# A two-layer diffusion trunk: other products for the first 256 feed-forward columns, two thirds of the second layer's modulation on TensorE, other buffers for the last down weights

## The chip, the core and the metric

One NeuronCore of one Trainium2 chip runs the whole program, in one launch, on fp32 inputs. The metric is the device time of the core in microseconds (us). One execution was also profiled; its rows stand below.

## What is computed

Two trunk layers run over 640 tokens (512 sample tokens in tiles 0 to 3, 128 prompt tokens in tile 4). What matters here of the reference, for each layer:

```python
mod = silu(cond) @ w_mod + b_mod                     # six vectors of 1024, per condition
sh1, sc1, ga1, sh2, sc2, ga2 = split(mod, 6)
h = rmsnorm(x, g_pre1) * (1 + sc1) + sh1
proj = h @ w_in                                      # inputs of four mixers, and the gates
mix = sum_m(sigmoid(gate_m) * (branch_m @ w_br_m)) @ w_o
x = x + ga1 * rmsnorm(mix, g_post1)
h2 = rmsnorm(x, g_pre2) * (1 + sc2) + sh2
gt, up = split(h2 @ w_up, 2)                         # 2 x 2816 columns
x = x + ga2 * rmsnorm((silu(gt) * up) @ w_down, g_post2)
```

## The kernel before, in words

**Products.** Every fp32 operand is split into a high and a low part (ScalarE copies the high part, VectorE subtracts), and a product is the sum of three matmuls: high by high, high by low, low by high (`mm`, L135; transposes are L140). `wchunk` (L143 to 152) loads weights into a `raw` buffer (three of them) and splits them into `whi` and `wlo`.

**Feed-forward.** The 22 blocks of 128 columns are taken in `FGROUPS`: a group of two blocks, then five groups of four. For each pair of blocks `up_pair` (L1321) is called for the gate half and for the up half of `w_up`. It computes 256 columns by 640 tokens with Strassen's seven products instead of eight: each is a sum of weight blocks (made on VectorE, L1333, and split, L1352) by a sum of activation blocks. The tokens are cut into halves of 320 (`TH`), the depth of 1024 into two halves, so a product has 12 matmuls of 320 columns and a pair 84. The activation blocks lie in `hb`: `hb[1]` and `hb[2]` hold the first token half, `hb[3]` the second half's lower depth, and 5, 6, 7, 4 are sums that `combine` (L1294) makes tile by tile once the tiles 2, 3 and 4 of the second half are normed. After a group's pairs comes its down projection (10 outputs of 512 columns for five token tiles and two column halves).

**The head.** `ffn_head` (L1400) runs behind the output projection of the mixers and fills the time in which `post` (L1230) and `prenorm` (L361; its Square is L369) of the last tiles finish. It starts three pairs, (0,0), (0,1) and (1,0), as generators with products 1 and 2 of each, which need `hb[1]` and `hb[2]` alone; between them it pops from `self.late` the norms of tiles 3 and 4, and then the three `combine`s. The other products follow in `ffn`.

**Modulation.** A layer's six vectors come in three groups of 2048 columns. `mod_group` (L281) does a group on TensorE: 16 loads of 512 KB into `V` (two buffers), each followed by four matmuls of 32 rows by 256 columns, in four column strips of the array (`keep`, L218). `mod_group_v` (L305) does a group on VectorE: 64 operations of 128 by 512 (L319, L321), and a few closing matmuls. Layer 0's groups 1 and 2 go by `mod_group` during `gates(2)`. Layer 1's three groups go by `mod_group_v` as a filler in layer 0's feed-forward: one step for each `up_pair`, three for each weight chunk of a down projection (`step`, L1418).

**The last group.** For the last group of a layer all of the down weights are held, so that tile by tile (L1472 ff.) both column halves are finished, added up (L1481) and passed to `post`: the residual, the next layer's first norm, and the store of the output. The weights are two chunks in `whi`/`wlo` for the first column half, one more for the second, and two single blocks that `wchunk1` (L154) puts into `tg` and `cv`. `tg` has two buffers, and `post` also needs one: L1238 writes `tg<-acc,oh`.

A tile framework places the instructions: it orders each engine by data and buffer dependences, so a buffer that comes free later delays all that is to write it. All loads are issued by SyncE, in order.

Of the kernel before, what the change touches and what calls it, by code (L numbers as in the profile page):

```python
# [10 lines left out]
F32R = mybir.dt.float32r  # L11
# [7 lines left out]
KT = 8  # L19
# [10 lines left out]
HEAD = 1, 2, 5, 6, 3, 7, 4  # L30
# [9 lines left out]
TG = 648  # L40
# [67 lines left out]
class Step:  # L108
# [44 lines left out]

    def wchunk1(self, src, tags):  # L154

        nc = self.nc
        raw = self.t("raw", [128, 1024])[:, :512]
        self.dma.dma_start(raw, src.rearrange("p k c -> p (k c)"))
        hi, lo = (self.t(t, [128, TG], F32R)[:, :512] for t in tags)
        nc.scalar.activation(hi, raw, AF.Copy)  # L160
        nc.vector.tensor_tensor(lo, raw, hi, op=ALU.subtract)
        return hi.unsqueeze(1), lo.unsqueeze(1)
# [1067 lines left out]
    def post(self, i, t0, t1, s, G, xsrc, xdst, M, which, hh2):  # L1230
# [15 lines left out]
        if hh2 is not None:  # L1246
# [18 lines left out]
    def new_hb(self):  # L1265

        t = [self.t(n, [128, KT, NTOK], F32R).rearrange("p a t -> p (a t)") for n in ("hhi", "hlo")]
        blk = lambda x, j: x[:, j * SLOT:j * SLOT + SLOT].rearrange("p (k t) -> p k t", k=4)
        return {p: (blk(t[0], j), blk(t[1], j)) for j, p in enumerate((1, 2, 3, 5))}
# [51 lines left out]
    def up_pair(self, l, c0, hb, silu, E, order, tag="raw"):  # L1321
# [5 lines left out]
        for q in range(2):  # L1327
            r = self.t(tag, [128, 1024 if tag == "raw" else SLOT])[:, :1024].rearrange("p (k c) -> p k c", k=4)
# [3 lines left out]
        s1 = None  # L1332
        tt = lambda o, x, y, op: nc.vector.tensor_tensor(o, x, y, op=op)  # L1333
        done = set()

        def operand(p):
            nonlocal s1
            if p == 5 or p in (6, 7, 3) and 5 not in done:
                s1 = self.t("dt", [128, 512]).rearrange("p (k c) -> p k c", k=4)
                tt(s1, A21, A22, ALU.add)  # L1340
                done.add(5)
            if p in (6, 7, 3) and 6 not in done:
                tt(A21, A11, A21, ALU.subtract)
                tt(A11, s1, A11, ALU.subtract)
                done.add(6)
            if p == 3:
# [12 lines left out]
        for p in order:  # L1359
# [25 lines left out]
            if p in (3, 4) and {3, 4} <= set(order[:order.index(p) + 1]):  # L1385
# [6 lines left out]
            yield  # L1392
# [6 lines left out]

    def ffn_head(self, l, hb):  # L1400

        head = {}
        late = self.late
        self.late = []
# [202 lines left out]
```

## Time and profile before

| | us |
|---|---|
| three runs | 2465.18, 2472.25, 2473.31 (median 2472.25) |
| the profiled execution | 2471.39 |
| its span, first to last instruction | 2469.6 |
| TensorE busy | 2305.1 |
| VectorE busy | 1670.7 |
| ScalarE busy | 998.5 |
| GpSimd busy | 259.4 |

The mean granted clock of TensorE is 0.970 of full speed. TensorE is the busiest engine, but busy time is an average over stages: a stage's own limit is read from windows of it. A row of a window gives, after its stretch, each engine's busy time with its instructions in brackets, then the granted clock, the DMA engines' share and the rate. PEld is TensorE's weight load.

### The profile page before, as it was taken

How to read it: one execution, taken by the hardware profiler on the slowest of the kernel's cores; microseconds unless marked ns; L12 is line 12 of the kernel's file. 1: busy time of each engine (PE TensorE's matmuls, PEld its weight loads, DVE VectorE, ACT ScalarE, POOL GpSimd, SP SyncE). 2: the span in 40 equal slices, each digit the busy share in tenths (PEclk: the TensorE clock that was granted, in tenths of full speed). 3: DMA queues.
4: the chain of work that ended last, by engine and by line, in shares of the span. 5: the costliest groups of instructions: out<-in, count | busy, mean ns of one | idle time of the engine just before them, and what ended most of it. 6: DMA issues, size and time to landing. Idle time of an engine off the chain costs nothing. (4 is left out here: it accounts for less than half of the span.)

```text
span 2469.6 us, 38694 instructions
## 1 busy us (share of the span) xinstructions
PE 2305.1 (93%) x14822; PEld 2027.0 (82%) x14822; DVE 1670.7 (68%) x3546; ACT 998.5 (40%) x2076; POOL 259.4 (11%) x320
## 2 busy tenths in 40 slices
PE   7999999999996898889989999999999969999996
PEld 6877688979875877779978887889799759999995
DVE  4653788476458899997666646884764587666765
ACT  4442553232236524234344544532322356334442
POOL 0000203131030000000011011031310300000001
PEclk9999999999998999999989999999999979999998
DMA  9647033325342354553344121234253422222222
GB/s 264 162 126 226 29 91 87 98 58 129 123 146 91 111 167 137 168 158 97 94 122 112 37 57 51 86 88 101 58 145 110 148 86 77 86 83 89 86 85 94
DMA packets 316585, 269.45 MB, mean 109 GB/s; under 512 B 72096, under 2 KB 267296, under 8 KB 316400
## 3 DMA queue, kind: packets, MB, share of 16 engines
q1 hardware_dynamic: 316400, 266.98, 36.3%
q8 instruction: 117, 1.92, 0.3%
q14 instruction: 68, 0.56, 0.1%
HBM read 234.73 MB, written 32.20 MB: 108 GB/s over the span
## 5 line engine op out<-in xcount | busy, mean ns | idle before, releaser
L135 PE MATMUL psg<-hhi,wlo 128*128 128x384 f32 (+2 forms) x1632 | 509.8, 321 | 9.4 <-ACT wlo L1352 4.4
L135 PE MATMUL psg<-hhi,whi 128*128 128x384 f32 (+2 forms) x1600 | 502.3, 321 | 7.1 <-DVE tg L1186 5.6
L135 PE MATMUL psg<-hlo,whi 128*128 128x384 f32 (+2 forms) x1520 | 486.9, 320 | 0.0
L151 DVE TENSOR_TENSOR wlo<-raw,whi 128x1024 fp32r<-128x1024 f32 (+1 forms) x170 | 212.7, 1252 | 177.7 <-ACT whi L150 175.0
L135 PEld LDWEIGHTS psg<-hhi,wlo 128*128 128x128 f32 x1632 | 308.3, 191 | 23.0 <-issue 6.9
L135 PEld LDWEIGHTS psg<-hhi,whi 128*128 128x128 f32 x1600 | 300.9, 190 | 20.6 <-issue 8.1
L135 PEld LDWEIGHTS psg<-hlo,whi 128*128 128x128 f32 x1520 | 288.5, 190 | 16.2 <-issue 14.3
L150 ACT ACTIVATE whi<-raw 128x1024 fp32r<-128x1024 f32 (+1 forms) x170 | 179.6, 1058 | 212.5 <-PE psg L135 161.6
L135 PE MATMUL pss<-hhi,whi 128*128 128x320 f32 x512 | 133.9, 330 | 29.0 <-ACT whi L1352 13.4
L135 PE MATMUL pss<-hhi,wlo 128*128 128x320 f32 x544 | 134.1, 314 | 7.6 <-ACT hhi L1307 4.9
L1155 ACT ACTIVATE tg<-psg 128x384 f32<-128x384 f32 (+1 forms) x128 | 55.0, 431 | 196.1 <-PE psg L135 177.5
L321 DVE SCALAR_TENSOR_TENSOR P<-V,cs,P 128x512 f32<-128x512 f32 x168 | 119.2, 749 | 16.8 <-DMA V<-in_w_mod 16.3
L1352 ACT ACTIVATE wlo<-raw 128x512 fp32r<-128x512 f32 x118 | 73.1, 630 | 131.1 <-PE psc L135 63.7
L135 PE MATMUL psg<-oh,whi 128*128 128x384 f32 (+1 forms) x512 | 119.8, 318 | 4.3 <-DVE tg L1186 4.0
L135 PEld LDWEIGHTS pss<-hhi,whi 128*128 128x128 f32 x512 | 94.6, 202 | 34.1 <-DVE whi L1333 15.1
L135 PE MATMUL psg<-whi,U 128*128 128x512 f32 x356 | 117.2, 392 | 0.0
L1333 DVE TENSOR_TENSOR wlo<-raw,wlo 128x512 fp32r<-128x512 f32 x118 | 81.2, 689 | 47.7 <-ACT wlo L1352 47.1
L1188 POOL TENSOR_TENSOR acc<-acc,tg 128x640 f32<-128x640 f32 x48 | 85.2, 1779 | 248.7 <-DVE tg L1186 248.7
L135 PEld LDWEIGHTS pss<-hhi,wlo 128*128 128x128 f32 x544 | 95.5, 192 | 9.9 <-ACT hhi L1307 5.7
L1333 DVE TENSOR_TENSOR whi<-raw,whi 128x512 fp32r<-128x512 f32 x122 | 83.6, 689 | 29.3 <-ACT whi L1352 29.3
L135 PE MATMUL pss<-whi,U 128*128 128x512 f32 x304 | 101.8, 391 | 1.0 <-ACT U L167 1.0
L135 PEld LDWEIGHTS psg<-oh,whi 128*128 128x128 f32 x512 | 86.1, 190 | 12.9 <-DVE tg L1186 7.8
(578 smaller groups left out, 5114.1 us busy)
## 6 DMA issues: line engine op xcount, KB each, us to landing
raw<-in_w_in SPq DMA_DIRECT2D x86, 512.0 KB
raw<-in_w_up SPq DMA_DIRECT2D x80, 512.0 KB
V<-in_w_mod SPq DMA_DIRECT2D x96, 256.0 KB
raw<-in_w_down SPq DMA_DIRECT2D x42, 512.0 KB
V<-in_w_mod SPq DMA_DIRECT2D x32, 512.0 KB
raw<-in_w_o SPq DMA_DIRECT2D x16, 512.0 KB
xs<-V SPq DMA_DIRECT2D x15, 512.0 KB
V<-xs SPq DMA_DIRECT2D x15, 512.0 KB
```

Source lines behind the costliest of these rows:

```text
L135: return self.nc.tensor.matmul(out, lhsT, rhs, start=start, stop=stop, skip_group_check=True)
L150: nc.scalar.activation(hi, raw[:, :a * b], AF.Copy)
L151: nc.vector.tensor_tensor(lo, raw[:, :a * b], hi, op=ALU.subtract)
L321: nc.vector.scalar_tensor_tensor(acc[:, s, :], raw, self.cs[:, k, s:s + 1], acc[:, s, :], op0=ALU.mult, op1=ALU.add)
L1155: self.nc.scalar.activation(tg[:, o:o + sz], p, AF.Tanh, scale=0.5)
L1188: nc.gpsimd.tensor_tensor(a, a, tg, op=ALU.add)
L1333: tt = lambda o, x, y, op: nc.vector.tensor_tensor(o, x, y, op=op)
L1352: nc.scalar.activation(hi, src, AF.Copy)
```

## The change

1. **The first 256 columns.** `ffn_head` no longer starts three pairs. It loads four chunks of 128 columns (blocks 0 and 1, gate and up) with `wchunk`, and multiplies each with the first token half (`fm_half`, 24 matmuls of 320 columns); norms of tiles 3 and 4 are popped after the first and the second. The new `ffn_first` then multiplies the same chunks with the second token half, from `hb[0]` (new, in two `U` buffers) and `hb[3]`, and pops a `combine` after each of the first three. Block products are eight here rather than seven, and pair (1,0) no longer begins in the head.
2. **Modulation.** In layer 0's feed-forward the filler is group 0 alone, one step for each `up_pair`. Groups 1 and 2 of layer 1 are done by `mod_group` in layer 1's `gates(2)`, as layer 0's are.
3. **The last weights.** The last group's fourth chunk goes whole into the two `T` buffers; `wchunk1` is gone, and with it the weights in `tg` and `cv`.
4. `norm_blocks` fills `hb[0]` too, and `more_hb` moves to the end of the head.

```diff
@@ post @@
-                self.late.append(lambda: (self.more_hb(hh2), self.combine(i, h32, hh2)))
+                self.late.append(lambda: self.combine(i, h32, hh2))
...
-                self.late.insert(2 * i - 6, lambda: self.h32.__setitem__(i, norm()))
+                self.late.insert(i - 3, lambda: self.h32.__setitem__(i, norm()))
@@ new_hb @@
+        hb[0] = tuple(self.t("U", [128, SLOT], F32R).rearrange("p (k t) -> p k t", k=4) for _ in range(2))
@@ norm_blocks @@
-                if second and q == 0:
-                    continue
-                hi, lo = hb[3 if second else 1 + q]
+                hi, lo = hb[3 * q if second else 1 + q]
@@ the head @@
+    def fm_half(self, out, w, b0, b1):
+        for k in range(KT):
+            for y, (a, b) in enumerate(((0, 0), (0, 1), (1, 0))):
+                self.mm(out, w[a][:, k, :], (b1 if k >= 4 else b0)[b][:, k % 4, :], k == 0 and y == 0, k == KT - 1 and y == 2)
...
     def ffn_head(self, l, hb):
-        for j, (n, up) in enumerate(((0, 0), (0, 1), (1, 0))):
-            E = self.pair_tiles(n, up)
-            g = self.up_pair(l, up * D_FF + n * 256, hb, not up, E, HEAD, ("raw", "U", "V")[j])
-            head[n, up] = g, E
-            next(g)
-            next(g)
-            if late:
-                late.pop(0)()
-        while late:
-            late.pop(0)()
+        for j, (n, up) in enumerate(((0, 0), (0, 1), (1, 0), (1, 1))):
+            ch = self.up_chunk(l, up * D_FF + n * 128, ("whi", "wlo") if j < 3 else ("oh", "oh"))
+            p = self.ps("s" if up else "g")[:, :TH]
+            self.fm_half(p, ch, hb[1], hb[2])
+            head[n, up] = ch, p
+            if j in (0, 1):
+                self.late.pop(0)()
+        self.more_hb(hb)
         return head
+    def ffn_first(self, head, hb):
...
+        for n in range(2):
+            out = {}
+            for up in range(2):
+                ch, p = head[n, up]
+                q = self.ps("s" if up else "g")[:, :TH]
+                self.fm_half(q, ch, hb[0], hb[3])
+                out[up] = (t1, p), (t2, q)
+                if self.late:
+                    self.late.pop(0)()
...
+            self.split(hi[:, n, :], lo[:, n, :], s)
@@ ffn @@
-            parts = {"hi": [], "lo": []}
+            parts = {"hi": [], "lo": []} if gi else self.ffn_first(head, hb)
...
                         ch = mk(k, co)
-                        step(3)
...
-            chs.append([(mk(0, 512), (0, 1), (0, 1))])
-            chs[1] += [(self.wchunk1(wd[:, f0 + k:f0 + k + 1, 512:1024], ("tg", "cv")), (0,), (k,)) for k in range(2, nf)]
+            chs = [[(mk(k, co, ("T", "T") if k and co else ("whi", "wlo")), (0, 1), (k, k + 1)) for k in range(0, nf, 2)]
+                   for co in (0, 512)]
@@ run @@
-            if l == 0:
-                self.bg = chain(*(self.mod_group(M, g, "c", "c") for g in (1, 2)))
+            self.bg = chain(*(self.mod_group(M, g, "c", "c") for g in (1, 2)))
...
-                filler = chain(*(self.mod_group_v(Mn, g, "o", "t") for g in range(3)))
+                filler = self.mod_group_v(Mn, 0, "o", "t")
```

How the change moves instructions shows at three places. In the rows below a name before the arrow is written, names behind it are read, and numbers tell buffers apart.

TensorE in the head of layer 0, before: the last of 48 matmuls on `hb[1]` and `hb[2]` (`hhi`, `hlo`), for two pairs, then the transposes of tile 3's norm (written to `pst` and `psc`), twelve more matmuls, the transposes of tile 4, and twelve more.

```order
L135 MATMUL pss_7750<-hhi_7103,whi_7747 128x320
L140 MATMUL pst_7704<-cst_63,P_7690 128x128 x4
L140 MATMUL psc_7705<-cst_63,P_7690 128x128 x4
L135 MATMUL psg_7791<-hhi_7103,wlo_7788 128x320
...
L135 MATMUL psg_7791<-hhi_7103,wlo_7788 128x320
L140 MATMUL pst_7836<-cst_63,P_7822 128x128 x4
L140 MATMUL psc_7837<-cst_63,P_7822 128x128 x4
L135 MATMUL pss_7808<-hhi_7103,whi_7805 128x320
```

TensorE at the same place now:

```order
L134 MATMUL psg_7794<-hhi_7103,wlo_7791 128x320
L139 MATMUL pst_7699<-cst_63,P_7685 128x128 x4
L139 MATMUL psc_7700<-cst_63,P_7685 128x128 x4
L134 MATMUL pss_7825<-hhi_7103,oh_7821 128x320
...
L134 MATMUL pss_7825<-hhi_7103,oh_7822 128x320
L139 MATMUL pst_7766<-cst_63,P_7752 128x128 x4
L139 MATMUL psc_7767<-cst_63,P_7752 128x128 x4
L134 MATMUL pss_7825<-hhi_7103,oh_7821 128x320
...
L134 MATMUL pss_7825<-hhi_7103,oh_7822 128x320
L134 MATMUL psg_7864<-U_7105,whi_7656 128x320
```

Of the first token half's 96 matmuls 72 now stand ahead of tile 3's transposes (48 before), and 18 more ahead of tile 4's (twelve before); from the row with `U` on come the products with the second token half.

VectorE in layer 0's feed-forward, with the filler (`P<-V,cs,P`) between operands of `up_pair`, before:

```order
L1333 TENSOR_TENSOR raw_8486<-raw_8486,raw_8484 128x4x128
L1333 TENSOR_TENSOR wlo_8593<-raw_8486,wlo_8593 128x512
L321 SCALAR_TENSOR_TENSOR P_8331<-V_8611,cs_218,P_8331 128x512
L1333 TENSOR_TENSOR whi_8577<-raw_8486,whi_8577 128x512
L1333 TENSOR_TENSOR tg_8483<-tg_8483 128x320
L321 SCALAR_TENSOR_TENSOR P_8331<-V_8611,cs_218,P_8331 128x512
L321 SCALAR_TENSOR_TENSOR P_8331<-V_8615,cs_218,P_8331 128x512
L1333 TENSOR_TENSOR tg_8482<-tg_8482,pss_8510 128x320
L321 SCALAR_TENSOR_TENSOR P_8331<-V_8615,cs_218,P_8331 128x512
```

and now:

```order
L310 SCALAR_TENSOR_TENSOR P_8249<-V_8387,cs_218,P_8249 128x512 x2
L310 SCALAR_TENSOR_TENSOR P_8249<-V_8529,cs_218,P_8249 128x512 x2
L1323 TENSOR_TENSOR wlo_8196<-raw_8121,wlo_8196 128x512
L310 SCALAR_TENSOR_TENSOR P_8249<-V_8533,cs_218,P_8249 128x512
L1323 TENSOR_TENSOR whi_8214<-raw_8123,whi_8214 128x512
L310 SCALAR_TENSOR_TENSOR P_8249<-V_8533,cs_218,P_8249 128x512
L1323 TENSOR_TENSOR wlo_8230<-raw_8123,wlo_8230 128x512
L310 SCALAR_TENSOR_TENSOR P_8249<-V_8663,cs_218,P_8249 128x512 x2
L1323 TENSOR_TENSOR whi_8264<-raw_8259,whi_8264 128x512
L1323 TENSOR_TENSOR dt_8263<-raw_8259,raw_8261 128x512
```

Line 310 is L321 in the numbering of before, L1323 is L1333. The filler's rows stand as close together as before, but there are 64 operations rather than 192: they reach from row 1180 to row 1350 of VectorE's order, those of before from row 1213 to row 1555. Between these ends now lie the first down projection, the whole of the next group (four `up_pair`s and its down projection) and three `up_pair`s more.

VectorE at the end of layer 1, before: the addition of the last tile's first half (`oh<-oh,psg`), and only then the L1238 of tiles 0 to 3, two at a time.

```order
L1481 TENSOR_TENSOR oh_19726<-oh_19726,psg_23313 128x512
L245 SCALAR_TENSOR_TENSOR rr_23297<-rs_u_23301,rr_23297 128x1
L1238 TENSOR_TENSOR tg_23135<-acc_19722,oh_23066 128x512
L1238 TENSOR_TENSOR tg_23188<-acc_19723,oh_23066 128x512
L1244 SCALAR_TENSOR_TENSOR V_23132<-tg_23135,rr_23138,V_23132 128x512
L1244 SCALAR_TENSOR_TENSOR V_23185<-tg_23188,rr_23191,V_23185 128x512
L1238 TENSOR_TENSOR tg_23241<-acc_19724,oh_23066 128x512
L1238 TENSOR_TENSOR tg_23294<-acc_19725,oh_23066 128x512
L1481 TENSOR_TENSOR oh_19726<-oh_19726,psg_23330 128x512
```

VectorE at the end of layer 1 now, tile 0 (L1484 is L1481, L1227 is L1238, L1232 and L1233 are L1243 and L1244):

```order
L1484 TENSOR_TENSOR acc_19557<-acc_19557,psg_22969 128x512
L1484 TENSOR_TENSOR acc_19557<-acc_19557,psg_22986 128x512
L1227 TENSOR_TENSOR tg_23003<-acc_19557,oh_22940 128x512
L1230 TENSOR_TENSOR ss_23007<-o_s_3487_22968 128x1
...
L1232 SCALAR_TENSOR_TENSOR V_23000<-acc_19557,rr_23006,V_23000 128x512
L1233 SCALAR_TENSOR_TENSOR V_23000<-tg_23003,rr_23006,V_23000 128x512
L1484 TENSOR_TENSOR acc_19558<-acc_19558,psg_23039 128x512
L1227 TENSOR_TENSOR tg_23056<-acc_19558,oh_22940 128x512
```

Tile 0's `tg` is now written, and its output finished, before tile 1's second half is added; in layer 0's last group it is the same.

## Rows read from the trace of the kernel before

**Rows 1.** The page, part 1: busy us, share of the span, instructions.
```profile
PE 2305.1 (93%) x14822; PEld 2027.0 (82%) x14822; DVE 1670.7 (68%) x3546; ACT 998.5 (40%) x2076; POOL 259.4 (11%) x320
```

**Rows 2.** Windows, layer 1, one group of four column blocks: engines' busy us, clock, DMA.
```profile
2112.90:2189.40 76.50, 76.50 (x458) 71.80 (x457) 51.59 (x81) 32.57 (x58) 0.00 (x0) 1.00 0.26 83
```

**Rows 3.** Windows, same columns: first down's end to last matmul, layers 0 and 1.
```profile
831.70:1277.70 446.00, 406.38 (x2316) 364.59 (x2315) 371.79 (x601) 167.36 (x304) 5.79 (x12) 0.97 0.42 132
2066.80:2447.00 380.20, 379.69 (x2256) 354.99 (x2255) 257.23 (x422) 165.73 (x303) 5.64 (x5) 1.00 0.26 81
```

**Rows 4.** The page, part 5: line, engine, tiles, count, busy, mean ns, idle before.
```profile
L321 DVE SCALAR_TENSOR_TENSOR P<-V,cs,P 128x512 f32<-128x512 f32 x168 | 119.2, 749 | 16.8 <-DMA V<-in_w_mod 16.3
```

**Rows 5.** Windows, same columns, layer 0's feed-forward with and without the filler.
```profile
1000.00:1100.00 100.00, 86.04 (x480) 74.77 (x481) 93.28 (x152) 32.75 (x59) 0.00 (x0) 0.98 0.49 154
1180.00:1260.00 80.00, 80.00 (x471) 74.06 (x470) 55.05 (x90) 35.15 (x65) 1.90 (x9) 1.00 0.32 98
```

**Rows 6.** Timeline, TensorE, head of layer 0: start, us, instruction, idle before and releaser.
```profile
763.31 0.57 PE L135 MATMUL psg<-hhi,wlo 128*128 128x320 f32 x2 [1.40 <-ACT hhi L1290]
...
770.71 0.31 PE L135 MATMUL pss<-hhi,whi 128*128 128x320 f32 x1
776.88 1.12 PE L140 MATMUL pst<-cst,P 128*128 128x128 f32 x4 [5.86 <-ACT P L369]
...
786.76 0.66 PE L140 MATMUL pst<-cst,P 128*128 128x128 f32 x4 [2.08 <-ACT P L369]
...
798.24 0.64 PE L135 MATMUL pss<-hlo,wlo 128*128 128x320 f32 x1 [0.58 <-DVE hlo L1303]
...
818.39 0.62 PE L135 MATMUL pss<-whi,U 128*128 128x512 f32 x2
...
831.68 0.31 PE L135 MATMUL pss<-hhi,wlo 128*128 128x320 f32 x1
```

**Rows 7.** Windows, heads of layers 0 and 1.
```profile
762.00:800.00 38.00, 20.42 (x96) 17.84 (x97) 35.16 (x92) 21.58 (x45) 0.76 (x1) 0.75 0.17 56
1996.00:2033.00 37.00, 19.99 (x90) 17.00 (x90) 33.31 (x89) 21.50 (x45) 0.76 (x1) 0.69 0.16 58
```

**Rows 8.** Chain of waits, layer 1: start, us, engine, tile, line, instructions.
```profile
2010.81 3.50 DMA V<-in_w_up
...
2150.72 3.51 PE psg L135 x24
```

**Rows 9.** Windows of line 218 alone, layer 0's gates.
```profile
130.00:245.00 115.00, 22.04 (x256) 6.61 (x256) 0.99 0.62 187
```

**Rows 10.** Line 218 there: what its engine waited for (us, times).
```profile
  DMA V<-in_w_mod: 7.4, 13
```

**Rows 11.** Timeline, TensorE, from layer 0's last matmul into layer 1.
```profile
1277.73 0.40 PE L135 MATMUL psg<-tg,U 128*128 128x512 f32 x1
1286.23 1.11 PE L140 MATMUL pst<-cst,P 128*128 128x128 f32 x4 [8.10 <-ACT P L369]
...
1290.37 0.78 PE L135 MATMUL psg<-whi,hhi 128*128 128x496 f32 x1 [2.17 <-ACT hhi L386]
```

**Rows 12.** Windows: start of layer 1's projection; after the last matmul.
```profile
1290.00:1318.00 28.00, 24.12 (x102) 17.97 (x102) 21.68 (x70) 20.00 (x37) 6.36 (x5) 0.88 0.37 126
2447.00:2469.60 22.60, 0.42 (x2) 0.00 (x0) 11.43 (x22) 0.72 (x2) 0.81 (x1) 0.57 0.53 186
```

**Rows 13.** Timeline, all engines, after layer 1's last matmul.
```profile
2446.77 2.19 DVE L1238 TENSOR_TENSOR tg<-acc,oh 128x512 f32<-128x512 f32 x2 [1.06 <-PE psg L135]
...
2451.41 0.68 DVE L1481 TENSOR_TENSOR oh<-oh,psg 128x512 f32<-128x512 f32 x1
...
2454.52 0.16 DVE L245 SCALAR_TENSOR_TENSOR rr<-rs_u,rr 128x1 f32<-128x1 f32 x1
...
2464.50 0.75 DVE L1243 SCALAR_TENSOR_TENSOR V<-oh,rr,V 128x512 f32<-128x512 f32 x1 [4.77 <-DMA V<-xs]
2465.95 0.33 SPq L1245 DMA_DIRECT2D out_y_prompt<-V  x1
```

More of the change, by code (lines that the diff above doesn't have):

```diff
@@ L1268, in new_hb @@
         blk = lambda x, j: x[:, j * SLOT:j * SLOT + SLOT].rearrange("p (k t) -> p k t", k=4)
-        return {p: (blk(t[0], j), blk(t[1], j)) for j, p in enumerate((1, 2, 3, 5))}
+        hb = {p: (blk(t[0], j), blk(t[1], j)) for j, p in enumerate((1, 2, 3, 5))}
+        hb[0] = tuple(self.t("U", [128, SLOT], F32R).rearrange("p (k t) -> p k t", k=4) for _ in range(2))
+        return hb
     def more_hb(self, hb):
@@ L1319, in combine, with up_pair @@
         parts(4, t6)
-    def up_pair(self, l, c0, hb, silu, E, order, tag="raw"):
+    def up_pair(self, l, c0, hb, silu, E):
         nc = self.nc
@@ L1331, in up_pair @@
         (A11, A21), (A12, A22) = ((r[:, :, 0:128], r[:, :, 128:256]) for r in raw)
-        s1 = None
+        s1 = self.t("dt", [128, 512]).rearrange("p (k c) -> p k c", k=4)
         tt = lambda o, x, y, op: nc.vector.tensor_tensor(o, x, y, op=op)
-        done = set()
         def operand(p):
-            nonlocal s1
-            if p == 5 or p in (6, 7, 3) and 5 not in done:
-                s1 = self.t("dt", [128, 512]).rearrange("p (k c) -> p k c", k=4)
+            if p == 5:
                 tt(s1, A21, A22, ALU.add)
-                done.add(5)
-            if p in (6, 7, 3) and 6 not in done:
+            elif p == 6:
                 tt(A21, A11, A21, ALU.subtract)
                 tt(A11, s1, A11, ALU.subtract)
-                done.add(6)
-            if p == 3:
+            elif p == 3:
                 tt(A12, A12, A11, ALU.subtract)
@@ L1358, in up_pair @@
         X = Y = Z = None
-        for p in order:
+        for p in PRODUCTS:
             whi, wlo = operand(p)
@@ L1384, in up_pair @@
                 tt(eA[:, t2], eA[:, t2], Z, ALU.add)
-            if p in (3, 4) and {3, 4} <= set(order[:order.index(p) + 1]):
+            elif p == 4:
                 if silu:
@@ L1417, in ffn, with step @@
     def ffn(self, l, hb, head, M, Mn, xsrc, xdst, hh2, filler):
-        def step(k=1):
-            for _ in range(k if filler is not None else 0):
+        def step():
+            if filler is not None:
                 next(filler, None)
@@ L1427, in ffn @@
             nf = f1 - f0
-            parts = {"hi": [], "lo": []}
-            for n in range(f0 // 2, f1 // 2):
+            parts = {"hi": [], "lo": []} if gi else self.ffn_first(head, hb)
+            for n in range(f0 // 2, f1 // 2) if gi else ():
                 Es = []
                 for up in range(2):
-                    if (n, up) in head:
-                        g, E = head[n, up]
-                    else:
-                        E = self.pair_tiles(n, up)
-                        g = self.up_pair(l, up * D_FF + n * 256, hb, not up, E, PRODUCTS)
-                    for _ in g:
-                        pass
+                    E = self.pair_tiles(n, up)
+                    self.up_pair(l, up * D_FF + n * 256, hb, not up, E)
                     Es.append(E)
```

28 lines of the change are left out of this document (13 added, 15 removed).

## The prediction

> **What bounds the kernel now.** I read the page first: TensorE is busy 93% of the span, VectorE 68% [rows 1]. That average says "TensorE-bound", so the next view is windows over stages, to find where TensorE is not. In layer 1's feed-forward a group of four column blocks takes 76.50 us, TensorE is busy for all of it at full clock, and VectorE needs 51.59 of it [rows 2]. There nothing but fewer matmuls helps. The other stages are compared with that one.
>
> Layer 0's feed-forward does the same from its first down projection on, but takes 446.0 us where layer 1 takes 380.2 [rows 3], 65.8 us more. The clock (0.97) is not it; VectorE is: in layer 0 it also carries the modulation filler, 168 operations of 749 ns and 24 of the first kind [rows 4]. While the filler runs VectorE is busy 93.28 of 100 us and TensorE 86.04; after it TensorE is busy 80 of 80 [rows 5]. So the reader sees VectorE set the pace there, with `up_pair` waiting for its operands.
>
> Three short places are left. In the head TensorE finishes the first 48 matmuls, then waits 5.86 us for the norm of tile 3, later for tile 4, and runs steadily only from 798.24 [rows 6]; in 38 us it is busy 20.42, at clock 0.75, and layer 1 looks the same [rows 7]. Between the layers it waits 8.10 us behind the last matmul, then 2.17 [rows 11]. At the end 22.6 us pass after the last matmul [rows 12], and the timeline shows why: L1238 of the first tiles begins there, because its `tg` has been full of weights [rows 13].
>
> **The price of a matmul.** 24 matmuls of 320 columns take 3.51 us back to back [rows 8], 0.146 each. A group's down projection of 60 matmuls took 831.68 − 818.39 = 13.3 us [rows 6].
>
> **The head, twice.** The matmul count until the first down projection ends is the same, 192 before and now: eight block products for two blocks make 192, seven made 168, with 24 for pair (1,0) on top. Those 24 are not done any more and come back later, in pair (1,0) itself: +3.5 us a layer. What can be won is the stall. In 762 to 800, 96 matmuls at 0.146 would take 14.0; 38 less 1.3 before the first leaves 22.7 of stall and low clock [rows 7]. Now 96 matmuls need only the first half, 14.0 us from 763.31: they reach 777.3, so tile 3's wait (transposes at 776.88) is covered. Tile 4's transposes come 9.9 us after tile 3's [rows 6], with VectorE busy 35.16 of 38 [rows 7]: operand sums and the `combine` of tile 2 stand between. Now the two norms follow each other, and only splits of plain weight chunks compete. I put tile 4's 5 us earlier, half of the 9.9, at 781.8, and its blocks for the second token half 6 us behind, at 788 (before, it took 11.5 us to 798.24, with combines in it). Then 14.0 for 96 matmuls, 2.2 for product and split (three operations of some 0.7, as L1481 [rows 13]) and 13.3 for the down projection end at 817.5, against 831.7: 14.2 less 3.5, some **11 us a layer, 22 in all**. Bounds for a layer: −3.5 if tile 4 is as late as before, 19.2 if no stall remains (22.7 − 3.5).
>
> **The filler.** It falls to 56 operations of 749 ns, 41.9 us, and eight of the cheaper kind. The order puts them into the first down projection, one group and three pairs: 13.3 + 76.5 + 36.9 (three times 84 matmuls of 0.146) = 127 us of TensorE, in which VectorE has 127 × 51.59 / 76.5 = 85.6 of its own [rows 2]. That makes some 130 us: still slightly too much. If all is even, 4 us stay; if it bunches as it did, a third of 65.8, 22. I take 11: **−55 us** (bounds −44 and −66).
>
> **Modulation on TensorE, layer 1.** Layer 0 shows the same 32 loads and 128 matmuls: TensorE is busy 22.04 us with them (two records each) [rows 9] and waited 7.4 us for their data [rows 10]. Layer 1's mixers are bound by TensorE as layer 0's are, so nothing hides it: between 22.0 and 29.4, **+26 us**. The Trainium skill speaks against this part: "TensorEngine Tiling (Array Packing)", section "Tiling Modes", says that a change of tiling mode drains TensorE, and each of the 32 sets is a change to column strips and back. By that rule the sum would have the upper end, 29, rather than 22; the rows of layer 0 contain whatever the drain costs inside the busy time, and no row shows it by itself.
>
> **Last weights: between the layers.** With `tg` free, tile by tile's `post` and the next layer's norms run beside the last matmuls, and the first transposes too. The stretch from the last matmul to the first of the projection, 1278.1 to 1290.4, holds 12.3 us, of which about 1 is transposes that must be done anyway; in the 28 us after it TensorE idles 3.9 and runs at 0.88 clock [rows 11, 12], some 2.9 more. Together 18: **−18 us**. Bounds: 8, if only the first wait goes, and 19.
>
> **Last weights: the end.** Now only tile 4's `post` lies behind the last matmul: 0.4 of matmul, 3.3 from its addition to its scale (2451.41 to 2454.68), 1.4 for two operations, and 3.65 from the last store's issue to the span's end [rows 13], 8.7 in all against 22.6 [rows 12]. That is 13.9; I take **−13**, since the fourth chunk can only be split once the last pair has let go of `T`, and keep 8 as the low bound, should the loads of the residual be late (4.77 us of waiting before [rows 13]).
>
> The `hb[0]` copies and `more_hb` cost nothing of their own: the copies replace operand sums on the same VectorE and GpSimd, and without that cover they would be part of the head's 6 us. Weight loads by shorter runs are hidden as the DMA engines are at 0.17 in the head [rows 7]; not hidden, the chunks' landing would delay the head's first matmul, which is inside its low bound.
>
> **Sum.** −22 − 55 + 26 − 18 − 13 = −82. The profiled execution took 2471.39, 0.9 under the median of the runs; 2471.4 − 82 = **2389 us**.
>
> **Rivals.**
> - *The filler still saturates.* Bunched into 127 us, VectorE stays the pace there, and 22 of 65.8 stay. For: VectorE needs 130 of 127. Against: the load is thinner than before. 2389 + 11 = 2400.
> - *The heads give nothing.* VectorE and ScalarE, not TensorE's order, set when tile 4 is ready. For: VectorE is busy 35.16 of 38 [rows 7]. Against: operand sums leave that stretch. 2389 + 22 = 2411, or 2418 with the 3.5 of each layer.
> - *The freed `tg` hands nothing over.* The chunk in `T` waits for the last pair, tile 0's second half with it, and each tile's `post` slides behind the matmuls again. 2389 + 31 = 2420. Against: the order has tile 0's output ahead of tile 1's second half.
> - *Everything fits.* No filler stall, heads at their bounds: 2389 − 11 − 16 = 2362.
> - *Slower: SyncE's queue in layer 1.* The 32 loads of 512 KB go through two `V` buffers, in order ahead of the loads of the gates' weights; a load that waits for its buffer holds those behind it, and TensorE, which has all of the mixers' work there, waits for each landing. The nearest row is a landing that the chain shows exposed, 3.50 us [rows 8]: 32 × 3.5 + 22 = 134 instead of 26, 2389 + 108 = 2497. It decides from (108 − 22) / 32 = 2.7 us of exposure a load, 108 being the other gains. Against: layer 0 runs the same loads and waits 7.4 us in all [rows 10].
>
> That the change does not do what it says is excluded by the order of instructions, which shows all three parts.
>
> **Chances.** Forecast as summed, within its bounds, 0.53; filler saturates 0.12; heads give nothing 0.10; `tg` hands nothing over 0.07; everything fits 0.07; two of the bad ones together, 2430 to 2455, 0.05; these with dear loads, ending at about no change, 0.03; slower 0.03. A measurement of this kernel tells some 0.3%, 7 us, from no change: faster by more than that 0.94, within it 0.03, slower 0.03. The range runs from everything fits to the third rival, 2360 to 2421; outside lie the last three cases and the edges of the others, less than 2 in 10.
>
> **What would show it.** Right: layer 0's feed-forward from its first down on takes 390 to 395 us, VectorE busy above 0.9 only in its first 130; the mixers of layer 1 grow by 22 to 29 us, with column-strip matmuls busy 22 and waits of under 8 for `V`; the two transposes in the head come within some 5 us of each other, and the first down ends about 54 us after the head's first matmul (68.4 before); L1227 (L1238 before) runs during the last group; some 9 us follow the last matmul. Wrong: any of these missing by more than 10 us, above all waits for `V` or for gate weights in layer 1's `gates(2)`, or second-half matmuls that wait for `U` until the old time.

## The result and the profile after

The changed kernel takes **2395.68 us** (median of four runs, 2394.38 to 2404.82) against 2472.78 of the kernel before (four runs, 2465.18 to 2475.47): a ratio of 0.9701, interval 0.9668 to 0.9733. The forecast was 2389. The profiled execution took 2396.94, 74.5 us under that of before. The page's head and first part, as in [rows 1]:

```profile
span 2395.1 us, 38984 instructions
...
PE 2291.1 (96%) x15094; PEld 2020.9 (84%) x15094; DVE 1577.0 (66%) x3370; ACT 984.2 (41%) x2046; POOL 280.5 (12%) x326
```

TensorE is busy 14.0 us less, though it runs 272 instructions more. The mean granted clock went from 0.970 to 0.989, and at a low clock the same matmul is busy for longer: between 787.80 and 790.00 of this trace the granted clock is 0.50 and matmuls of 320 columns start 0.27 us apart, where at 1.00 they start 0.146 apart [rows 8].

Both traces can be cut at the same landmarks, at the starts of the instructions named. The stretches between them, in us:

| stretch | before | after | difference | forecast |
|---|---|---|---|---|
| start to the head's first matmul, layer 0 | 763.31 | 760.71 | −2.6 | 0 |
| head of layer 0, to its first down's end | 68.4 | 56.1 | −12.3 | −14.2 |
| from there to layer 0's last matmul | 446.0 | 398.0 | −48.0 | −55 + 3.5 |
| from there to the first gate's eviction (L1155, now L1144) | 95.4 | 79.7 | −15.8 | −18 |
| from there to the head of layer 1 | 624.1 | 648.7 | +24.6 | +26 |
| head of layer 1 | 69.5 | 57.2 | −12.3 | −14.2 |
| from there to the last matmul | 380.2 | 384.0 | +3.8 | +3.5 |
| behind the last matmul | 22.6 | 10.7 | −11.9 | −13 |

The first line is not put down to the change: TensorE's order is the same up to the head, and the traces of the runs below, which leave that stretch alone, have it between 754.0 and 766.9. The rows behind the others follow.

Windows over both feed-forwards, as in [rows 3], and over layer 0's with and without the filler, as in [rows 5]:

```profile
816.80:1214.80 398.00, 390.74 (x2316) 362.32 (x2315) 303.10 (x511) 176.07 (x325) 8.15 (x6) 1.00 0.35 111
2000.40:2384.40 384.00, 383.08 (x2280) 358.65 (x2279) 265.19 (x431) 166.45 (x303) 5.99 (x4) 1.00 0.28 88
820.00:920.00 100.00, 97.25 (x592) 91.36 (x590) 92.35 (x153) 41.15 (x78) 0.00 (x0) 1.00 0.48 150
920.00:1180.00 260.00, 259.49 (x1572) 243.28 (x1573) 177.39 (x282) 112.43 (x202) 0.00 (x0) 1.00 0.30 93
```

Layer 0 now takes 14 us more than layer 1 instead of 65.8. While the filler runs (its last operation starts at 927.3) TensorE misses 2.75 us in 100; afterwards it is busy 259.49 of 260. VectorE is still at 92% in that first stretch.

TensorE's timeline in the head of layer 0, as in [rows 6]:

```profile
760.71 0.64 PE L134 MATMUL psg<-hhi,whi 128*128 128x320 f32 x1 [2.75 <-ACT hhi L1280]
...
776.55 0.66 PE L139 MATMUL pst<-cst,P 128*128 128x128 f32 x4
...
778.21 0.31 PE L134 MATMUL pss<-hhi,oh 128*128 128x320 f32 x1
781.00 0.52 PE L134 MATMUL psg<-U,whi 128*128 128x320 f32 x1 [2.48 <-ACT U L1280]
...
787.77 0.64 PE L134 MATMUL psg<-U,whi 128*128 128x320 f32 x1 [5.71 <-POOL U L1282]
...
803.13 0.40 PE L134 MATMUL pss<-whi,U 128*128 128x512 f32 x1
...
816.83 0.31 PE L134 MATMUL psg<-hhi,wlo 128*128 128x320 f32 x1
```

112 matmuls and transposes run from 760.71 to 778.21 with no wait for tile 3 or tile 4, whose transposes start at 776.55. Then TensorE waits twice for blocks in `U`, the second time 5.71 us for GpSimd. The second token half runs from 787.77, 27.1 us after the head's start; the forecast had 24.7.

Layer 1's strip matmuls by themselves, as in [rows 9], and what they waited for, as in [rows 10]:

```profile
1290.00:1450.00 160.00, 20.44 (x256) 6.21 (x256) 1.00 0.47 143
```

```profile
  DMA V<-in_w_mod: 5.0, 12
```

20.4 us of busy time and 5.0 of waits: layer 0's picture again, and close to the 24.6 of the table.

TensorE between the layers, as in [rows 11]:

```profile
1215.06 0.40 PE L134 MATMUL psg<-whi,hhi 128*128 128x496 f32 x1
...
1220.00 0.49 PE L134 MATMUL psg<-wlo,hhi 128*128 128x496 f32 x1 [1.62 <-DVE wlo L150]
...
1226.81 0.49 PE L134 MATMUL psg<-whi,hhi 128*128 128x496 f32 x1 [0.71 <-ACT hhi L375]
```

The projection's first matmul starts 0.23 us behind the last down matmul (1214.83): the 8.10 us wait for the norm is gone, because the first tiles' transposes ran among the last down matmuls. Two of them waited there for the copy that scales the norm (L358, L369 before, which is this copy and not the Square):

```profile
1197.57 0.66 PE L139 MATMUL pst<-cst,P 128*128 128x128 f32 x4 [1.17 <-ACT P L358]
...
1207.70 1.05 PE L139 MATMUL pst<-cst,P 128*128 128x128 f32 x4 [1.95 <-ACT P L358]
```

Behind the last down matmul there are short waits for weights and for later tiles.

VectorE behind the last matmul, as in [rows 13]:

```profile
2386.74 0.68 DVE L1484 TENSOR_TENSOR oh<-oh,psg 128x512 f32<-128x512 f32 x1
...
2389.99 0.16 DVE L234 SCALAR_TENSOR_TENSOR rr<-rs_u,rr 128x1 f32<-128x1 f32 x1
...
2390.91 0.75 DVE L1233 SCALAR_TENSOR_TENSOR V<-tg,rr,V 128x512 f32<-128x512 f32 x1
```

Only tile 4's addition, scale and two operations remain, some 4.9 us, and the store.

### The profile page after: what moved, and what is told of

Same layout as the page of the kernel before. It is cut to its first block, busy times and chain, and to the rows that moved or that the text cites. A ratio compares the mean times of both kernels' runs of the same rounds, so it can differ in the third digit from the quotient of the medians.

```text
span 2395.1 us, 38984 instructions
## 1 busy us (share of the span) xinstructions
PE 2291.1 (96%) x15094; PEld 2020.9 (84%) x15094; DVE 1577.0 (66%) x3370; ACT 984.2 (41%) x2046; POOL 280.5 (12%) x326
## 3 DMA queue, kind: packets, MB, share of 16 engines
q8 instruction: 119, 1.95, 0.3%
## 5 line engine op out<-in xcount | busy, mean ns | idle before, releaser
L134 PE MATMUL psg<-hhi,whi 128*128 128x384 f32 (+2 forms) x1648 | 515.9, 320 | 11.7 <-DVE tg L1175 5.6
L134 PE MATMUL psg<-hlo,whi 128*128 128x256 f32 (+2 forms) x1568 | 504.0, 321 | 0.1
L150 DVE TENSOR_TENSOR wlo<-raw,whi 128x1024 fp32r<-128x1024 f32 (+1 forms) x176 | 219.5, 1248 | 208.2 <-ACT whi L149 205.5
L134 PEld LDWEIGHTS psg<-hhi,whi 128*128 128x128 f32 x1648 | 310.7, 190 | 22.9 <-DVE tg L1175 7.1
L134 PEld LDWEIGHTS psg<-hlo,whi 128*128 128x128 f32 x1568 | 298.2, 190 | 15.6 <-issue 13.2
L1144 ACT ACTIVATE tg<-psg 128x384 f32<-128x384 f32 (+1 forms) x128 | 54.9, 431 | 222.0 <-PE psg L134 203.1
L1323 DVE TENSOR_TENSOR wlo<-raw,wlo 128x512 fp32r<-128x512 f32 x120 | 82.8, 690 | 64.8 <-ACT wlo L1337 64.2
L134 PE MATMUL pss<-hhi,whi 128*128 128x320 f32 x504 | 122.9, 309 | 0.0
L134 PE MATMUL pss<-hhi,wlo 128*128 128x320 f32 x504 | 122.7, 308 | 0.0
L1488 POOL TENSOR_TENSOR acc<-acc,oh 128x512 f32<-128x512 f32 x8 | 11.3, 1409 | 814.4 <-ACT dt L1487 808.4
L1323 DVE TENSOR_TENSOR whi<-raw,whi 128x512 fp32r<-128x512 f32 x120 | 82.3, 689 | 33.9 <-ACT whi L1337 33.9
L134 PEld LDWEIGHTS psg<-oh,whi 128*128 128x128 f32 x512 | 85.0, 188 | 14.2 <-DVE tg L1175 6.9
L1337 ACT ACTIVATE whi<-raw 128x512 fp32r<-128x512 f32 x120 | 75.4, 631 | 41.5 <-DVE raw L1323 27.4
L134 PEld LDWEIGHTS pss<-hhi,whi 128*128 128x128 f32 x504 | 87.3, 188 | 0.0
```

The lines of the kernel that those rows point to most:

```text
L134: return self.nc.tensor.matmul(out, lhsT, rhs, start=start, stop=stop, skip_group_check=True)
L150: nc.vector.tensor_tensor(lo, raw[:, :a * b], hi, op=ALU.subtract)
L1144: self.nc.scalar.activation(tg[:, o:o + sz], p, AF.Tanh, scale=0.5)
L1337: nc.scalar.activation(hi, src, AF.Copy)
L1488: nc.gpsimd.tensor_tensor(y, y, G[0 if i < 4 else 1][:, 0:512], op=ALU.mult)
```

## The experiments

Times are medians; the changed kernel is 2395.7. Each kernel was timed beside the kernel before on the same chip, whose medians were 2469.8 to 2471.0. The intervals of the ratios are 0.002 to 0.003 to either side, 4 to 8 us, so a difference of a few us between two medians says little by itself; the same stretches as in the table, cut out of each run's trace, are given beside it where a reading rests on them.

**One part undone at a time.** *1. The head of before* in the changed kernel:

```diff
-            parts = {"hi": [], "lo": []} if gi else self.ffn_first(head, hb)
+            parts = {"hi": [], "lo": []}
...
+                    if (n, up) in head:
+                        g, E = head[n, up]
```

> The changed kernel with the head of before (three pairs begun by seven products) and the other two parts kept. Ledger theory (the parts add up): the two heads took 68.4 and 69.6 us before and 56.1 and 57.2 in the changed kernel, less the 24 matmuls that come back in each layer (3.5 us): the change's head is worth 17.4 us, so 2395.7 + 17 = 2413. Rival, that the head's gain is only the order of the two norms and overlaps with what the other parts free: 2396 to 2400.

2412.4 (2409.8 to 2415.9; ratio to before 0.9761, 0.9743 to 0.9779). The heads are worth 16.7 us, close to the 17.6 that the table gives for them (two times 12.3, less two times 3.5).

*2. The modulation of before:*

```diff
-                filler = self.mod_group_v(Mn, 0, "o", "t")
+                filler = chain(*(self.mod_group_v(Mn, g, "o", "t") for g in range(3)))
...
                         ch = mk(k, co)
+                        step(3)
...
+            if l == 0:
                 self.bg = chain(*(self.mod_group(M, g, "c", "c") for g in (1, 2)))
```

> The changed kernel with all three modulation groups of layer 1 on VectorE again, in layer 0's feed-forward, and no strip matmuls in layer 1. Ledger theory: layer 0's feed-forward gets back some 50 us (48.1 were seen, plus the 3.5 of pair (1,0)), layer 1's mixers lose 24.6: 2395.7 + 27 = 2422, with VectorE busy above 0.9 in layer 0's feed-forward. Rival, that VectorE's load now fits because the step in the head and the freed tg loosen it: less than 10 us slower, or faster, down to 2371.

2421.3 (0.9795, 0.9778 to 0.9812), 25.6 us slower. Layer 1's mixers take 623.5 us again, 25 less than in the changed kernel, so by the medians the two groups on VectorE cost 25.6 + 24.6 = 50.2 us in layer 0. In the trace layer 0's feed-forward, from the first down's end to its last matmul, takes 445.1 us against 398.0: 47.1 of them are there.

*3. The last weights of before:*

```diff
-            chs = [[(mk(k, co, ("T", "T") if k and co else ("whi", "wlo")), (0, 1), (k, k + 1)) for k in range(0, nf, 2)]
-                   for co in (0, 512)]
+            chs.append([(mk(0, 512), (0, 1), (0, 1))])
+            chs[1] += [(self.wchunk1(wd[:, f0 + k:f0 + k + 1, 512:1024], ("tg", "cv")), (0,), (k,)) for k in range(2, nf)]
```

> The changed kernel with the fourth chunk of the last weights in tg and cv again. Ledger theory: the stretch behind layer 0's last matmul takes back 15.8 us and the end 11.9, less some 3 to 5 that the posts beside the last matmuls now cost layer 0's last group: 2395.7 + 24 = 2420, and L1227 of the first tiles starts behind the last matmul again. Rival, that the transition's gain comes from the lighter filler in front of it: only the end's 12 us come back, 2408.

2416.9 (0.9781, 0.9763 to 0.98): 21.2 us. The waits of TensorE at the end of layer 0 show the old one back:

```profile
PE pst L139 <- ACT P L368: 8.0, 1, 8.0
```

16.7 + 25.6 + 21.2 = 63.5 of the 77 us. The stretches of the table give 17.6, 26.9 and 27.7 for the same three parts, so the last weights are worth 6 us less by undoing them. This run's trace has these 6: the two stretches behind the last matmuls take 17.9 and 12.2 us more than in the changed kernel, but layer 0's feed-forward takes 391.3 instead of 398.0, 6.7 less, and its last group no longer holds the transposes of layer 1's norm, with their waits of 1.17 and 1.95 us and the granted clock of 0.52 behind the second (1207.70 to 1211.20). So the new last weights pay for a part of their gain in the group before. What is left of the 77 can't be told from scatter.

**The head.** *4. The subtraction into `hb[0]` on VectorE:*

```diff
-                eng = nc.gpsimd if q == 0 else nc.vector
+                eng = nc.gpsimd if q == 0 and not second else nc.vector
```

> The changed kernel with the low part of hb[0] subtracted on VectorE instead of GpSimd. In the changed kernel's head TensorE waits 5.7 us for GpSimd's last subtraction into U, which takes 6.69 us where the one of half its size took 1.28. Theory: that subtraction is what the second token half waits for; on VectorE it takes 0.7 us, and each head gains 4 to 5 us: 2387. Rival: the combines and copies of tile 4 are ready no earlier, so TensorE waits for them or for VectorE instead, and less than 2 us are won: 2394 to 2396.

2386.9 (0.9656, 0.9631 to 0.9681): 8.8 us faster than the changed kernel by the medians; in the trace the heads take 50.8 and 50.7 us instead of 56.1 and 57.2, 11.8 less. In its timeline of TensorE the two waits of 2.48 and 5.71 have become one:

```profile
774.11 0.31 PE L134 MATMUL pss<-hhi,oh 128*128 128x320 f32 x1
777.59 0.63 PE L134 MATMUL psg<-U,whi 128*128 128x320 f32 x1 [3.17 <-ACT U L1280]
```

*5. The order of the norms alone,* in the kernel before:

```diff
-                self.late.insert(2 * i - 6, lambda: self.h32.__setitem__(i, norm()))
+                self.late.insert(i - 3, lambda: self.h32.__setitem__(i, norm()))
```

> The kernel before with one edit: the norms of tiles 3 and 4 are popped ahead of the combine of tile 2, as in the changed kernel; seven products, old modulation, old last weights. Theory: the head's gain comes from more matmuls that need only the first token half, and from second-half blocks that need no combine; the order of the norms alone leaves the products 5, 6, 7 and 4 waiting for the same sums on VectorE: within 5 us of before, 2466 to 2474. Rival: the order of the norms is the gain; two heads of some 10 to 12 us: 2447 to 2452.

2470.6 against 2470.2 (1.0005, 0.9991 to 1.002): nothing. The head's gain needs the other products.

*10. 24 matmuls moved out of the cover:*

```diff
-            p = self.ps("s" if up else "g")[:, :TH]
-            self.fm_half(p, ch, hb[1], hb[2])
+            p = self.ps("s" if up else "g")[:, :TH] if j < 3 else None
+            if j < 3:
+                self.fm_half(p, ch, hb[1], hb[2])
```

> The changed kernel with the first token half of the fourth chunk multiplied in the second part of the head instead of ahead of it: the same matmuls, 24 of them moved behind the wait for tile 4's blocks. Theory: the matmuls that need only the first token half cover the wait, so moving 24 of them (3.5 us) out of the cover costs up to that in each head: 2395.7 + 5 to 7 = 2401 to 2403. Rival: TensorE's fewer matmuls in front of tile 4's transposes let its blocks be ready earlier by as much, and nothing is lost: 2394 to 2397.

2412.7 (2405.7 to 2424.6; 0.9757, 0.9726 to 0.9787): slower, as the theory has it, but at more than twice the price. In its profile the heads take 62.6 and 62.6 us instead of 56.1 and 57.2, so 12 of the 17 us are there. Two times 3.5 are the moved matmuls. The theory had not counted the rest: the wait for GpSimd's subtraction grew from 5.71 to 7.74 us, because that subtraction took 9.10 us instead of 6.69 (the last section shows why). The other 5 are within this kernel's wide scatter.

**The filler.** *6. The loads without the operations:*

```diff
-                filler = self.mod_group_v(Mn, 0, "o", "t")
+                filler = chain(self.mod_group_v(Mn, 0, "o", "t"), self.mod_loads(1), self.mod_loads(2))
...
+                self.dma.dma_start(raw, self.I["w_mod"][1, k * 128:k * 128 + 128, c:c + 512])
+                self.nc.gpsimd.tensor_copy(self.t("mlj", [128, 1]), raw[:, 0:1])
```

> The changed kernel, with the loads of modulation groups 1 and 2 (64 of 256 KB) issued again in layer 0's feed-forward as extra traffic, read by nothing but a one-column copy on GpSimd; VectorE gets no operation more. Theory: VectorE's operations held TensorE in layer 0's feed-forward, not the loads or SyncE's queue: 2396 to 2400. Rival: the loads, by their buffers and the queue, were the cost: two thirds of the 65.8 us come back, 2440.

2422.6 (0.9799, 0.9778 to 0.9819): 27 us slower, between the two. The waits of VectorE name the weights of the pairs:

```profile
DVE dt L1333 <- DMA raw<-in_w_up: 33.2, 10, 9.3
```

33.2 us in ten waits, where the changed kernel has 10.8 in twelve and the kernel before 3.5 in three. VectorE's operations no longer pace the loads, and they fill SyncE's queue: between 906 and 934 the trace of SyncE has two to seven of them from one load of `w_up` to the next, and SyncE waits for their `V` buffers. So this run shows a cost that the kernel before did not have, and does not say what its cost was.

*9. The operations without the loads:*

```diff
-                for s in range(2):
+                for z, s in [(z, s) for z in range(3) for s in range(2)]:
```

> The changed kernel with every VectorE operation of the filler's one group done three times on the same loaded tile: 192 operations as before the change, but 32 loads of 256 KB instead of 96. Nothing else is done more (the sums are too large by it). Theory: VectorE's operations were what held TensorE in layer 0's feed-forward before the change; 128 more of them bring back what the two groups cost there, 48 to 52 us, with few waits for loads: 2440 to 2448. Rival: the loads did it, by SyncE's queue in front of the pairs' weights, as in the run with loads alone; without loads the operations fit beside TensorE: at most 15 us, 2411.

2404.4 (0.9737, 0.9713 to 0.9761): 8.7 us by the medians, 10.2 in the trace (408.2 against 398.0 in layer 0's feed-forward). My theory falls: 128 operations more do not cost 50 us. Windows from 820 and from 920:

```profile
820.00:920.00 100.00, 94.75 (x562) 88.13 (x561) 97.84 (x161) 41.20 (x76) 0.00 (x0) 0.98 0.34 104
920.00:1020.00 100.00, 98.07 (x589) 92.02 (x588) 97.97 (x162) 43.78 (x80) 0.00 (x0) 0.98 0.32 98
```

VectorE is busy 98 of 100 and TensorE still 95 and 98. A full VectorE is no loss by itself. The operations lie spread here, over the 305 us from 803 to 1108; before the change the same number stood in 281 (830 to 1111), in which TensorE did less (86 of 100 [rows 5]).

*11. Larger loads,* in the second run's kernel:

```diff
-                self.dma.dma_start(raw, I["w_mod"][l, k * 128:k * 128 + 128, c:c + 512])
+                if k % 2 == 0:
...
+                    self.dma.dma_start(big, I["w_mod"][l, k * 128:k * 128 + 256, c:c + 512].rearrange("(a p) c -> p a c", p=128))
```

> The second run's kernel (all three modulation groups of layer 1 on VectorE, 2421.3 us) with one edit: the filler loads two depth blocks at a time, 48 loads of 512 KB instead of 96 of 256 KB into the same two V buffers; the same bytes and the same VectorE operations. The ninth run showed that the operations alone cost some 9 us, so the rest of their 50 is tied to the loads. Theory: VectorE takes its instructions in order and stands still when a load of 256 KB, which feeds only two operations (1.5 us), has not landed (13.0 us of such waits in the second run, 16.3 before the change), and every weight split behind it stands too; with four operations a load the two buffers cover the landing: 15 to 25 us won, 2396 to 2406. Rival: the bytes, or the places that the loads take in SyncE's queue in front of weight loads, are the cost; the bytes are the same: 2414 to 2424.

2408.9 (0.9743, 0.9717 to 0.9769): 12.4 us won, between both. The waits for `V` fell from 13.0 to 3.6 us; the loads' landing was a part, not the rest. In the trace layer 0's feed-forward falls from 445.1 to 437.4 us, by 7.7, so of the 12.4 some 5 are not seen there and may be scatter.

*12. The same filler, spread:*

```diff
                         ch = mk(k, co)
-                        step(3)
+                        step(2)
```

> The eleventh run's kernel (three groups on VectorE, loads of 512 KB, 2408.9 us) with one number changed: two filler steps for each down chunk instead of three, so that the 48 steps reach over some four and a half groups of layer 0's feed-forward instead of three; the same loads, operations and bytes. Theory: what is left of the filler's cost is its density: 272 us of feed-forward held all of its 126 us and VectorE had no slack for late splits (two waits of TensorE for one line's splits made 16.0 us); spread out, 8 to 15 us come back: 2394 to 2401. Rival: each load and operation has its price wherever it stands: 2405 to 2412.

2381.2 (2377.1 to 2383.9; 0.9629, 0.9606 to 0.9652): 27.8 us won by one number, twice what was expected (25.9 in the trace: layer 0's feed-forward takes 411.5 us instead of 437.4). With no modulation of layer 1 on TensorE at all, this is faster than the changed kernel. The same windows of the eleventh run, then its longest waits of TensorE, then the windows and the same waits of this one:

```profile
820.00:920.00 100.00, 86.15 (x481) 77.67 (x480) 96.38 (x160) 33.02 (x61) 0.00 (x0) 0.91 0.52 160
920.00:1020.00 100.00, 89.01 (x528) 81.70 (x527) 96.84 (x160) 35.53 (x66) 0.00 (x0) 0.95 0.52 167
```

```profile
PE psg L134 <- DVE wlo L1325: 16.0, 2, 8.5
```

```profile
820.00:920.00 100.00, 98.92 (x606) 91.11 (x605) 98.25 (x166) 42.68 (x80) 0.00 (x0) 1.00 0.51 161
920.00:1020.00 100.00, 97.51 (x587) 92.02 (x586) 96.97 (x158) 43.65 (x80) 0.00 (x0) 0.98 0.48 148
```

```profile
PE psg L134 <- DVE wlo L1325: 5.1, 2, 3.1
```

VectorE is as busy in both (96 to 98 of 100), but the filler has 91.5 us of its 200 in the eleventh run, 74.5 in this one and 78.5 in the ninth. What dense means shows in the timeline of VectorE and TensorE of the eleventh run, at the first of the two waits:

```profile
907.27 1.41 DVE L312 SCALAR_TENSOR_TENSOR P<-V,cs,P 128x512 f32<-128x512 f32 x2
909.01 2.74 DVE L312 SCALAR_TENSOR_TENSOR P<-V,cs,P 128x512 f32<-128x512 f32 x4 [0.33 <-DMA V<-in_w_mod]
911.67 1.28 DVE L1475 TENSOR_TENSOR acc<-acc,pss 128x512 f32<-128x512 f32 x2
912.86 0.68 DVE L1475 TENSOR_TENSOR oh<-oh,psc 128x512 f32<-128x512 f32 x1
913.46 0.68 DVE L1325 TENSOR_TENSOR wlo<-raw,wlo 128x512 fp32r<-128x512 f32 x1
914.20 0.90 PE L134 MATMUL psg<-hhi,wlo 128*128 128x320 f32 x2 [7.43 <-DVE wlo L1325]
```

TensorE waits from 906.77. VectorE does eight filler operations (the first two, from 906.47 on, are not shown) and three additions, and only then the split that TensorE needs; the second wait, 8.55 us, has eight as well. In the twelfth run the two waits for this line's splits are 2.02 and 3.08 us, and no filler operation falls into them. From the first down's end to layer 0's last matmul TensorE misses 32.6 us in the eleventh run and 12.8 in the twelfth, and its granted clock, 0.91 in the first window, is 1.00. The loads are spread with the operations: VectorE's waits for the pairs' weights fell from 6.7 to 0.9 us, so a part may be theirs. Spreading all three groups with loads of 256 KB was not tried.

**The modulation on TensorE.** *7. Every strip matmul twice:*

```diff
-                       for j in range(4)])
+                       for z in range(l + 1) for j in range(4)])
```

> The changed kernel with every strip matmul of layer 1's modulation issued twice in a row (four strips, then the same four again; the sums come out twice as large), with no load and no set more. Theory: the 24.6 us that layer 1's mixers grew by are TensorE's own time in these matmuls (20.4 us busy) and little else: 20 us more, 2416. Rival: it is the waits for the loads and the change between strips and the full array, which doubling inside a set does not repeat: at most 8 us more, 2404.

2415.0 (0.9766, 0.975 to 0.9783): 19.3 us more. Its windows row of line 207:

```profile
1290.00:1500.00 210.00, 36.49 (x512) 14.78 (x512) 1.00 0.38 114
```

16.05 us more busy (36.49 against 20.44). So some 16 to 20 of the 24.6 are the matmuls' own time, and 4 to 8 are waits and what goes with a set of four strips.

*8. Two groups on VectorE:*

```diff
-                filler = self.mod_group_v(Mn, 0, "o", "t")
+                filler = chain(*(self.mod_group_v(Mn, g, "o", "t") for g in (0, 1)))
...
                         ch = mk(k, co)
+                        step()
...
-            self.bg = chain(*(self.mod_group(M, g, "c", "c") for g in (1, 2)))
+            self.bg = chain(*(self.mod_group(M, g, "c", "c") for g in ((1, 2) if l == 0 else (2,))))
```

> The kernel of the fourth run (low part of hb[0] on VectorE) with modulation group 1 of layer 1 back on VectorE in layer 0's feed-forward, one step for each pair and one for each down chunk, and only group 2 on TensorE. Theory: spread over the whole feed-forward VectorE carries two groups: 257 us of its own and 92 of filler in 380. Half of the 24.6 us on TensorE goes, some 4 us of waits come: 2386.9 - 12 + 4 = 2379. Rival: the filler bunches and VectorE sets the pace again, 18 us: 2393.

2379.6 (2376.0 to 2381.4; 0.9619, 0.9602 to 0.9635), the lowest median here, with the fourth run's edit in it, and what its theory forecast. The twelfth run is within its interval without that edit; the two together were not tried.

## Why the prediction was right, and where not

- **What bounds the kernel**: as read. The gain came from the stretches in which TensorE waited; in layer 1's feed-forward only the 3.5 us of pair (1,0) came on top (3.8 measured). One reading was too quick: "the clock (0.97) is not it". As many matmuls, 2316, were busy 406.38 us in layer 0's feed-forward at a mean clock of 0.97 and are busy 390.74 at 1.00. So of the 48 us some 32 are waits, and some 16 are TensorE's own busy time, which fell as the waits went and the clock rose.
- **The heads**: forecast 22, measured 24.6 − 7 = 17.6 in the traces and 16.7 by the first run. The cover worked as forecast (tile 3's wait is gone; run 5 shows that the norms' order alone is worth nothing, run 10 that moving matmuls out of the cover costs at least their time), and tile 4's transposes came even earlier, 15.8 us after the head's start instead of 18.5. The step that failed is "the `hb[0]` copies and `more_hb` cost nothing of their own". The blocks for the second token half were forecast 6 us behind tile 4's transposes and came 11.2 behind, because GpSimd's copy is what they wait for; the fourth run gives 8.8 us back. The early norm made up for a part of this, and that is luck.
- **The filler**: forecast −55, measured −51.5 with the 3.5 taken out. That stretch also pays 6.7 us for the new last weights (run 3), so the filler's part is 47 (undone in run 2) to 58. The size was right: it came from the gap between the two layers, which does not ask for the cause. Its ground was only half right. "VectorE sets the pace" holds for the kernel before, but not because it has too much to do: the eleventh and twelfth run have the same work and differ by 27.8 us. Of the two groups' 47.1 us in layer 0's feed-forward, 7.7 went with larger loads (run 11), 25.9 with spreading (run 12), and 13.5 are left; operations without loads, nearly as far spread, cost 10.2 (run 9). Each is one trace, good to a few us. The row that misled was the busy share: 93 of 100 beside a slow TensorE [rows 5] looks like a limit, and 98 of 100 beside a fast one was possible.
- **Modulation on TensorE**: forecast 26, measured 24.6; doubling puts most of it on the matmuls' own time. The rule on tiling modes in the Trainium skill's "TensorEngine Tiling (Array Packing)", section "Tiling Modes", can at most explain part of the 4 to 8 us beyond them; no run shows a drain by itself. The slower rival had its place in the sixth run instead: loads that fill SyncE's queue do hold weights back, but in layer 1's gates TensorE waited for `V` 5.0 us in all, 0.16 a load, not the 2.7 from which on that rival would have decided.
- **Between the layers and the end**: forecast −18 and −13, measured −15.8 and −11.9; undoing both cost 21.2. The sum put at nothing what the norms and transposes cost where they went, in layer 0's last group: 6.7 us by run 3. Short waits for weights in the projection are not in it either.

The sum was −82, the profiled executions differ by 74.5. By stretches all five terms are a little smaller than forecast, none by more than 5 us. By parts the misses are larger: the last weights are worth 21 instead of 31, and GpSimd's copy costs 9 to 12 us that the forecast put at nothing. That the filler's stretch came out 3.5 us from its forecast, with the last weights' 6.7 in it, is in part luck.

## What to carry to other kernels

Background work on an engine that also feeds TensorE cost more by its density here than by its total: two modulation groups on VectorE cost some 13 us spread and 39 dense (runs 12 and 11 against the changed kernel, layer 0's feed-forward), and 24.6 on TensorE. So look first at how many background operations stand in a row in front of what TensorE needs next, spread them over the stretch that has slack, and only then think of moving them to the bounding engine. When the last uses of a buffer end a phase, ask which first use of the next phase waits for that buffer; other buffers for the last weights freed that chain here. And when new blocks are made for a product that waits for them, give the copy to the engine that finishes first in that stretch, not to the one that is idle on average.

## What the runs showed of the hardware

GpSimd's subtraction of 128 by 512 took 1.28 us at 777.44 and 6.69 us 3.6 us later. (Both have this shape; what was expected of the fourth run calls the first half the size.) The timeline of VectorE, GpSimd and TensorE of the changed kernel (start, us, engine, instruction):

```profile
777.44 1.28 POOL L1282 TENSOR_TENSOR U<-P,U 128x512 fp32r<-128x512 f32 x1 [15.11 <-ACT U L1280]
778.00 1.26 DVE L1282 TENSOR_TENSOR hlo<-P,hhi 128x512 fp32r<-128x512 f32 x1
...
780.50 0.68 DVE L1293 TENSOR_TENSOR P<-P,hlo 128x512 f32<-128x512 f32 x1
781.03 6.69 POOL L1282 TENSOR_TENSOR U<-P,U 128x512 fp32r<-128x512 f32 x1 [2.31 <-ACT U L1280]
781.10 0.68 DVE L1293 TENSOR_TENSOR P<-P,hhi 128x512 f32<-128x512 f32 x1
...
785.91 0.68 DVE L1293 TENSOR_TENSOR P<-hhi,P 128x512 f32<-128x512 f32 x1
...
787.77 0.64 PE L134 MATMUL psg<-U,whi 128*128 128x320 f32 x1 [5.71 <-POOL U L1282]
```

VectorE issues ten operations back to back from 780.50, each with two inputs in SBUF, the last ending at 786.59; GpSimd's ends at 787.72, 1.1 us later, near the 1.28 us of the first one, as if it had begun only then. In layer 1's head the same ten stand there, and GpSimd's takes 6.69 us again. In the tenth run the order of instructions puts fourteen in the place of the ten, the last ending at 795.38:

```profile
787.41 9.10 POOL L1282 TENSOR_TENSOR U<-P,U 128x512 fp32r<-128x512 f32 x1 [2.31 <-ACT U L1280]
```

Four operations 0.60 us apart are 2.41 us more, and GpSimd's subtraction takes 2.41 us more, in both heads. The other way round the rows fit too: at 777.44 GpSimd was first, and VectorE's subtraction of 128 by 512 beside it took 1.26 us, where the next one of its kind, at 781.70, took 0.68.

The Trainium skill's "SBUF — State Buffer", section "SBUF: two separate sides", says that a VectorE operation with two SBUF inputs and a GpSimd operation that reads SBUF hold one port pair in turn, each for its whole instruction. The trace agrees, and adds that GpSimd got no turn between ten, or fourteen, instructions of VectorE. No run shows the port pair itself. The runs show that GpSimd's time went with the length of VectorE's row, and the fourth run shows that the copy was the wait.
